# A hybrid encoder layer on one core: rounding copies on another engine, two rows from another ring, and one function table

## The chip, the cores and the metric

The kernel runs on one core of a Trainium2 chip, as one launch. The metric is the device time in microseconds (us) of that core. The kernel before was run three times: 2490.52 us is the median, 2490.19 the lowest and 2495.68 the highest. One more execution was taken with the hardware profiler; its rows are what the text argues from.

A core has five engines with a queue each, and each queue issues its instructions in order: TensorE (PE; its weight loads are listed as PEld), VectorE (DVE), ScalarE (ACT), GpSimd (POOL) and SyncE (SP, which here only starts transfers). An instruction that waits holds up everything behind it in its own queue.

## The reference, cut to what matters

One layer is applied to 1024 new rows (a prompt) and to 64 rows that continue a stream with a cache. The width is 1024.

```python
xn = rmsnorm(x); proj = xn @ w_in          # z | xBC | dt | q | k | v | g_ssm | g_att
y  = SSD_scan(silu(conv(xBC)), dt)         # 32 heads of 64, state 128, 4 groups
y  = rmsnorm_per_group(y * silu(z))
o  = subln(diff_attention(q, k, v))
x  = x + (sig(g_ssm) * (y @ W_bs) + sig(g_att) * (o @ W_ba)) @ W_out
h  = rmsnorm(x) @ w_up; ha, hb = split(h)  # 2 x 2816
x  = x + (silu(conv(ha)) * hb) @ w_down
```

Everything is float32. Keys, values, states and the convolutions' last rows are returned as well.

## The kernel before, in words

**Numbers in two parts.** All operands of the large products are kept as a high part `hi` (the value rounded to fp32r, the float32 form that PE multiplies at its fast rate) and a low part `lo` (value minus `hi`). A product of 128x128 blocks is three matmuls: hi x hi, hi x lo, lo x hi (`product`, L145 to L150). So each operand that is not a weight already on the way needs a rounding copy and a subtraction. `weights` (L130 to L142) loads a block of 128x1024, rounds it on ACT (L141) and subtracts on DVE (L142).

**Layout.** Channels lie on the partitions; the 1088 rows (1024 + 64) lie along the free axis, in three stretches `WIDE` of 384, 384 and 320 columns.

**Stages, in time.** 1. RMSNorm of x, then v and dt. 2. q and k. 3. Attention, head by head; between its steps the generator `filler` runs pieces of other work: the projections of z, xBC with its convolution, and the gates (`stream`, in the order `ORDER`, the gates 1 and 0 last). 4. The scan (`scan`, 4 groups by three stretches), with the rest of `filler` and then `branch_tiles` between its steps. 5. The second half of the state-space branch, then the output projection and the second norm. 6. The feed-forward part.

**The branches** (`branch`, L184 on). A branch product takes eight row tiles of 128 channels as the right operand, for each of the three stretches, and eight output tiles m, in the turns `TURNS`. The right operand is made by `branch_rows` (L161): for attention both parts come from DRAM ready-made; for the state-space branch each of the eight tiles is loaded into a staging row (L171), rounded into `b_hi` on ACT (L172) and subtracted into `b_lo` on DVE (L173). The state-space branch has two halves of 1024 channels. The first half is multiplied during the scan; ACT copies each accumulator out (L197, `b_g`) and ACT's own queue starts its store into `n_sc`. The second half's rows (y_sc[D:]) exist only after the scan; `last_rows(x)` calls `branch_rows` for stretch x just after the first half has used that stretch for the last time, since `b_hi` and `b_lo` have one buffer for each stretch. Loaded rows, the neighbours read for the sums (gates, `n_sc`, `m_sc`; L180) and the copied accumulators share one ring `b_r` of 11 rows of 128x384. There are three accumulators in turn in the scan, one "mx" and two "mm", and only the two "mm" after it.

**The norm after the scan.** For each group and stretch `gated` multiplies y by z (POOL, L735), ACT squares, POOL adds; `normed` sums over partitions on PE, and `rstd_of` (L221 to L225) makes the reciprocal root with Ln, Exp and Square on ACT. y then goes to `y_sc` by a store in SP's queue (L751). The same helper serves every norm, the second one (`norm`, L892 on) too.

**Function tables.** ACT evaluates functions from a set of tables that is loaded beforehand. The program loads one by hand at the start (L246, the set that holds both Ln and Exp); the compiler puts further loads wherever the set in place lacks the next function. Tanh serves the gates (L431), z and the convolution, Silu the feed-forward part (L1079).

**The feed-forward part** splits each product into quarters and needs seven products of sums instead of eight. The right operands (PARTS) come from `first_differences` and `last_differences`; the left ones from `left_parts` (L945): two loaded blocks of weights give four quarters q11, q12, q21, q22; POOL makes the sums s1 (L955), s2 (L956), q11 - q21 (L966) and q12 - s2 (L973); each of the seven is split on ACT (L860) and DVE (L861). Two column halves s = 0, 1 are handled alike. Tiles 0 and 1 are computed plainly (`pair_plain`), while the differences are made; tile 2 is the first with seven products (`pair`), and it takes them in the order 0, 2, 1, 3, 4, 5, 6. Its left operands are made at once by `left_of(2)`; those of each later tile are made step by step while the one before it is multiplied.

Rows of 128x544 come from rings: "fa" and "fb" of 8 rows, "fu" 4, "fp" 3, "fs" and "fh" 2. The normed x1 fills "fa" (quarters 0 and 2, which make half s = 0) and "fb" (quarters 1 and 3). Then "fs" holds the pair t2 of each half in `last_differences`, and after it the sums `ws1`, `ws2`; "fa" takes the split quarters `wh`, `wl`, eight rows for one tile.

**What sets the order.** The order of instructions in each queue isn't written out: a planner runs the whole program on simulated engines, takes what is ready by the order in which it was written (with a bonus for `tc.high_priority`), gives out the rows of the rings as they come free, and fixes the queues. A change in one place can so alter the order of everything behind it.

Of the kernel before, what the change touches and what calls it, by code (L numbers as in the profile page):

```python
# [11 lines left out]
AF = mybir.ActivationFunctionType  # L12
# [6 lines left out]
D = 1024  # L19
# [10 lines left out]
FT = DFF // P  # L30
NORM = (128, 256, 192, 192, 192, 128)
LN_EXP = "natural_log_exp_and_others"
# [43 lines left out]
def hybrid_layer(ctx: ExitStack, tc: tile.TileContext, xT, prm, cst, rope, wvd, win, wbs, wba, wout, wup, wdn,  # L76
                 ckT, cv, st0, yT, kT, v, ssm, conv, ffn):
    nc = tc.nc
    V, S, G, PE = nc.vector, nc.scalar, nc.gpsimd, nc.tensor
    act = S.activation  # L80
# [5 lines left out]
    def scratch(name, shape, dt=F32):  # L86
        return dram.tile(shape, dt, name=name, tag=name)
# [5 lines left out]
    o_sc, y_sc = scratch("o_sc", [2 * D, T]), scratch("y_sc", [2 * D, T])  # L93
# [58 lines left out]
    def project(block, evac):  # L152
        w_hi, w_lo = weights(block, KT, P)
        for (c, w), (hi, lo) in zip(WIDE, xn):
            ps = acc(w)
            product(ps, [(w_hi[:, k], w_lo[:, k], hi[:, k], lo[:, k]) for k in range(KT)])
            with tc.high_priority(quick or ahead):
                evac(ps, c, w)
            yield

    def branch_rows(stage, src, x):  # L161

        c, w = WIDE[x]
        hi, lo = (xn_pool.tile([P, KT, w], R32, name=f"b_{u}{x}", tag=f"{u}{x}") for u in ("hi", "lo"))
        for k in range(8):
            if stage is None:
                for u, t in enumerate((hi, lo)):
                    load(out=t[:, k].bitcast(F32), in_=src[D * u + P * k : D * u + P * (k + 1), c : c + w])
            else:
                t = stage()[:, :w]  # L170
                load(out=t, in_=src[P * k : P * (k + 1), c : c + w])  # L171
                S.copy(hi[:, k], t)  # L172
                V.tensor_tensor(out=lo[:, k], in0=t, in1=hi[:, k], op=ALU.subtract)  # L173
        return hi, lo

    def neighbours(side, gates, adds, m, c, w):
        tiles = []
        for d, r0 in ([(g_sc, gates)] if gates is not None else []) + [(d, 0) for d in adds]:
            t = side()[:, :w]
            load(out=t, in_=d[r0 + P * m : r0 + P * (m + 1), c : c + w])  # L180
            tiles.append(t)
        return tiles

    def branch(stage, side, src, wts, gates, adds, out, parts=None, loaded=None, then=None):  # L184

        parts = parts or [branch_rows(stage, src, x) for x in range(3)]
        for ms in TURNS:
            wt = [weights(wts[m], KT, P) for m in ms]
            for x, ((c, w), (hi, lo)) in enumerate(zip(WIDE, parts)):
                for m, (w_hi, w_lo) in zip(ms, wt):  # L190
                    beside = (loaded or {}).get((m, x)) or neighbours(side, gates, adds, m, c, w)
                    to = beside[0] if beside else side()[:, :w]
                    ps = acc(w)
                    product(ps, [(w_hi[:, k], w_lo[:, k], hi[:, k], lo[:, k]) for k in range(KT)])
                    with tc.high_priority(ahead):
                        if not beside:
                            S.copy(to, ps)  # L197
                        elif not adds:
                            V.scalar_tensor_tensor(to, to, 1.0, ps, ALU.add, ALU.mult)
                        else:  # L200
                            V.tensor_tensor(out=beside[1], in0=beside[1], in1=ps, op=ALU.add)
                    if adds:
                        V.scalar_tensor_tensor(to, to, 1.0, beside[1], ALU.add, ALU.mult)
                        V.tensor_tensor(out=to, in0=to, in1=beside[2], op=ALU.add)
                    out(m, c, to)
                    if then is not None and (m, ms) == (7, TURNS[-1]):
                        then(x)
                    yield

    def store(dst, start=load):  # L210
        return lambda m, c, t: start(out=dst[P * m : P * (m + 1), c : c + t.shape[1]], in_=t)
# [22 lines left out]
    s1 = ExitStack()  # L234
# [3 lines left out]
    def stat(w):  # L238
        t = ps1.tile([P, 512], F32, name="st", tag="st", bufs=3)
        return t[:, :w]  # L240
# [4 lines left out]
    with tc.tile_pool(name="nx", bufs=1) as nx:  # L245
        S.preload_act_table_set(LN_EXP)  # L246
        c = 0
        for x, w in enumerate(NORM):
            xc = nx.tile([P, KT, max(NORM)], F32, name="xc", tag="xc", bufs=3)
            ps = stat(w)  # L250
# [17 lines left out]
            for k in range(KT):  # L268
                xr = nx.tile([P, max(NORM)], F32, name="nxr", tag="nxr", bufs=NXR)
                (G if k % 3 == 2 else V).tensor_tensor(out=xr[:, :w], in0=xc[:, k, :w], in1=rs[:, :w], op=ALU.mult)  # L270
                hi, lo = (t[:, k, c % 384 : c % 384 + w] for t in xn[c // 384])
# [4 lines left out]
    def staged(name):  # L276
        return st.tile([P, 384], F32, name=name, tag="zr", bufs=ZR)
# [27 lines left out]
    with tc.tile_pool(name="qk", bufs=1) as qk:  # L305
# [5 lines left out]
        def row(name, w=T):  # L311
            t = qk.tile([P, T], F32, name=name, tag="qr", bufs=QR)
            return t[:, :w]
# [110 lines left out]
    extra = None  # L424
    cv_pool = tc.alloc_tile_pool(name="cv", bufs=1, side="right")

    def gate_tiles(tiles):
        for j in tiles:
            def evac(ps, c, w):
                gt = staged("gt")[:, :w]  # L430
                act(gt, ps, AF.Tanh, scale=0.5)  # L431
                load(out=g_sc[P * j : P * (j + 1), c : c + w], in_=gt)

            yield from project(win[B_G + j], evac)
# [44 lines left out]
    def stream():  # L479
        for kind, which in ORDER:  # L480
            yield from {"c": conv_tiles, "z": z_tiles, "g": gate_tiles}[kind](which)
        two = [gate_tiles([j]) for j in (1, 0)]
        for _ in WIDE:
            for u in two:
                yield next(u)
# [176 lines left out]
    with (tc.tile_pool(name="sin", bufs=1) as sin, tc.tile_pool(name="sp", bufs=1) as sp,  # L662
# [125 lines left out]
        def stage():  # L788
            return bs.tile([P, 384], F32, name="b_f", tag="b_r", bufs=BR)
# [3 lines left out]

        def branch_tiles():
            nonlocal bs
            cv_pool.release()
            st.release()
            bs = tc.alloc_tile_pool(name="bs", bufs=1, side="right")
            yield from branch(None, side, o_sc, wba, D, (), store(m_sc))
            yield from branch(stage, side, y_sc[:D], wbs[0], None, (), store(n_sc, S.dma_start), then=last_rows)  # L800

        def last_rows(x):
            assert scanned
            parts.append(branch_rows(stage, y_sc[D:], x))
            if x == 0:
                for m in TURNS[0]:
                    loaded[m, 0] = neighbours(side, 0, (n_sc, m_sc), m, *WIDE[0])

        parts, loaded, scanned = [], {}, False
        bs, late = None, chain(filler, branch_tiles())  # L810
        for i in scan():
            if i == BRANCH_AT and late is not None:
# [46 lines left out]
    def split(hi, lo, src):  # L859
        S.copy(hi, src)  # L860
        V.tensor_tensor(out=lo, in0=src, in1=hi, op=ALU.subtract)  # L861
# [80 lines left out]
            w.append((hi, lo))  # L942
        return w

    def left_parts(blocks):  # L945

        n = blocks[0].shape[1] // 2
        a = []
        for block in blocks:
            w = wp.tile([P, WMAX], F32, name="w_f", tag="w_f", bufs=2)  # L950
            load(out=w[:, : 2 * n], in_=block)
            a += [w[:, :n], w[:, n : 2 * n]]
        q11, q12, q21, q22 = a
        s1, s2 = (row("fs", name)[:, :n] for name in ("ws1", "ws2"))
        G.tensor_tensor(out=s1, in0=q21, in1=q22, op=ALU.add)  # L955
        G.tensor_tensor(out=s2, in0=s1, in1=q11, op=ALU.subtract)  # L956

        def own(src):
            hi, lo = (row("fa", name, R32)[:, :n] for name in ("wh", "wl"))
            split(hi, lo, src)  # L960
            return hi, lo

        yield own(q11)
        yield own(s2)
        yield own(q12)
        G.tensor_tensor(out=q21, in0=q11, in1=q21, op=ALU.subtract)  # L966
        yield own(q21)
        t = [wp.tile([P, WMAX], R32, name=name, tag=name, bufs=2) for name in ("w_hi", "w_lo")]
        for i, src in enumerate((s1, q22)):
            hi, lo = (x[:, 512 * i : 512 * i + n] for x in t)  # L970
            split(hi, lo, src)
            yield hi, lo
        G.tensor_tensor(out=s2, in0=q12, in1=s2, op=ALU.subtract)  # L973
        hi, lo = (wp.tile([P, WMAX], R32, name=name, tag=name, bufs=2)[:, :n] for name in ("w_hi", "w_lo"))
        split(hi, lo, s2)
        yield hi, lo
# [1 line left out]
    DOWN_AT = [sum(DOWN[:g]) for g in range(len(DOWN))]  # L978
    work = [(None, f) for f in range(FT)] + [(g, j) for g in range(len(DOWN)) for j in range(4)]

    def left_of(i):
        g, f = work[i]
        if g is None:
            return left_parts([wup[f], wup[f + FT]])
        n, o = P * DOWN[g], 1024 * DOWN_AT[g]
        return left_parts([wdn[:, o + n * m : o + n * (m + 1)] for m in (2 * f, 2 * f + 1)])

# [18 lines left out]
    left = {}  # L1006
# [229 lines left out]
        next(u)  # L1236
    for s in range(2):
        last_differences(s)
    left[2] = list(left_of(2))
    for u in pairs:  # L1240
        next(u)
    for i, (g, f) in enumerate(work[2:], 2):
# [123 lines left out]
```

## Time and profile before

| | |
|---|---|
| median of three runs | 2490.52 us (2490.19 to 2495.68) |
| profiled execution | 2488.03 us, of which the span from first to last instruction is 2486.2 us |
| PE busy | 2436.3 us, 98% of the span |
| DVE busy | 1589.3 us, 64% |
| ACT busy | 1181.0 us, 48% |
| POOL busy | 692.3 us, 28% |
| mean granted clock of PE | 0.996 |

How to read it: busy times are sums over the span; an engine that is idle while another one is the bound costs nothing. Names such as `mm<-b_hi,w_hi` stand for a tile written and the tiles read. L148 is line 148 of the kernel. A row of waits names who waited and for whom, with the total, the number and the longest. PEclk is the share of PE's full clock that was granted.

### The profile page before, as it was taken

How to read it: one execution, taken by the hardware profiler on the slowest of the kernel's cores; microseconds unless marked ns; L12 is line 12 of the kernel's file. 1: busy time of each engine (PE TensorE's matmuls, PEld its weight loads, DVE VectorE, ACT ScalarE, POOL GpSimd, SP SyncE). 2: the span in 40 equal slices, each digit the busy share in tenths (PEclk: the TensorE clock that was granted, in tenths of full speed). 3: DMA queues.
4: the chain of work that ended last, by engine and by line, in shares of the span. 5: the costliest groups of instructions: out<-in, count | busy, mean ns of one | idle time of the engine just before them, and what ended most of it. 6: DMA issues, size and time to landing. Idle time of an engine off the chain costs nothing. (4 is left out here: it accounts for less than half of the span.)

```text
span 2486.2 us, 44728 instructions
## 1 busy us (share of the span) xinstructions
PE 2436.3 (98%) x16958; PEld 2356.2 (95%) x16958; DVE 1589.3 (64%) x2735; ACT 1181.0 (48%) x2564; POOL 692.3 (28%) x712
## 2 busy tenths in 40 slices
PE   8999999999999999999999999999999999999999
PEld 7999999999999999998888899999999999999998
DVE  7326254865777667537666774655687777677765
ACT  6234343644565555437656663325543333344441
POOL 3000000000111001005324332003466666666435
PEclk9999999999999999999999999999999999999999
DMA  5217249454354353254688753655234333458874
GB/s 166 78 56 273 81 181 285 138 163 135 125 150 131 117 155 115 93 186 157 205 271 299 233 182 137 215 179 179 73 110 150 115 133 123 141 180 226 222 175 160
DMA packets 272152, 403.62 MB, mean 162 GB/s; under 512 B 32544, under 2 KB 206240, under 8 KB 271808
## 3 DMA queue, kind: packets, MB, share of 16 engines
q1 hardware_dynamic: 263872, 387.39, 48.2%
q0 software_dynamic: 4608, 8.91, 2.3%
q10 hardware_dynamic: 3456, 4.46, 0.5%
q8 instruction: 133, 2.18, 0.4%
q14 instruction: 83, 0.68, 0.1%
HBM read 267.11 MB, written 133.56 MB: 161 GB/s over the span
## 5 line engine op out<-in xcount | busy, mean ns | idle before, releaser
L148 PE MATMUL mm<-xn_hi,w_hi 128*128 128x384 f32 (+1 forms) x1416 | 469.9, 332 | 0.9 <-DVE zr L441 0.9
L150 PE MATMUL mm<-xn_hi,w_lo 128*128 128x384 f32 (+1 forms) x1416 | 467.7, 330 | 0.5 <-DVE w_lo L142 0.5
L149 PE MATMUL mm<-xn_lo,w_hi 128*128 128x384 f32 (+1 forms) x1416 | 466.5, 329 | 0.0
L148 PEld LDWEIGHTS mm<-xn_hi,w_hi 128*128 128x128 f32 x1416 | 266.2, 188 | 5.3 <-issue 2.0
L150 PEld LDWEIGHTS mm<-xn_hi,w_lo 128*128 128x128 f32 x1416 | 266.1, 188 | 2.9 <-issue 0.8
L149 PEld LDWEIGHTS mm<-xn_lo,w_hi 128*128 128x128 f32 x1416 | 266.2, 188 | 1.8 <-issue 0.6
L142 DVE TENSOR_TENSOR w_lo<-w_f,w_hi 128x1024 fp32r<-128x1024 f32 (+1 forms) x120 | 152.4, 1271 | 116.7 <-ACT w_hi L141 116.3
L1057 PE MATMUL mx<-n,wh 128*128 128x272 f32 x1092 | 209.0, 288 | 1.6 <-ACT u L1193 0.9
L1057 PE MATMUL mx<-m,w_hi 128*128 128x272 f32 x1050 | 201.8, 289 | 5.4 <-DVE down L1207 3.4
L141 ACT CAST w_hi<-w_f 128x1024 fp32r<-128x1024 f32 (+1 forms) x120 | 125.8, 1049 | 123.1 <-PE mm L149 68.5
L1057 PEld LDWEIGHTS mx<-n,wh 128*128 128x128 f32 x1092 | 171.4, 188 | 2.2 <-ACT u L1193 1.4
L1057 PEld LDWEIGHTS mx<-m,w_hi 128*128 128x128 f32 x1050 | 166.3, 190 | 6.3 <-DVE down L1207 4.1
L1057 PE MATMUL mx<-n,wl 128*128 128x272 f32 x546 | 157.2, 289 | 0.0
L148 PE MATMUL mm<-b_hi,w_hi 128*128 128x384 f32 (+1 forms) x448 | 147.9, 330 | 6.2 <-ACT b_g L197 6.2
L1057 PE MATMUL mx<-m,w_lo 128*128 128x272 f32 x525 | 151.9, 289 | 0.0
L150 PE MATMUL mm<-b_hi,w_lo 128*128 128x384 f32 (+1 forms) x448 | 146.5, 327 | 0.0
L149 PE MATMUL mm<-b_lo,w_hi 128*128 128x384 f32 (+1 forms) x448 | 146.3, 327 | 0.0
L559 ACT ACTIVATE p_t<-sc,mx 128x1024 f32<-128x1024 f32 (+5 forms) x144 | 106.1, 739 | 74.9 <-DVE mx L550 37.0
L470 DVE SCALAR_TENSOR_TENSOR cc<-pre,par,cc 128x384 f32<-128x384 f32 (+1 forms) x216 | 126.5, 586 | 23.7 <-ACT cc L468 18.6
L458 POOL COPY pre<-pre 128x3 f32<-128x3 f32 x48 | 13.2, 274 | 454.6 <-ACT pre L459 333.9
L860 ACT CAST w_hi<-ws 128x512 fp32r<-128x512 f32 (+1 forms) x64 | 38.9, 607 | 156.6 <-PE mx L1057 102.8
L697 POOL TENSOR_SCALAR_AFFINE_SELECT bc<-bc 128x1024 f32<-128x1024 f32 (+1 forms) x36 | 40.0, 1111 | 260.1 <-ACT e L684 260.1
(375 smaller groups left out, 6747.6 us busy)
## 6 DMA issues: line engine op xcount, KB each, us to landing
w_f<-in_win_dram SPq DMA_DIRECT2D x76, 512.0 KB, 3.7
w_f<-in_wup_dram SPq DMA_DIRECT2D x44, 512.0 KB, 3.6
hr<-q_sc SPq DMA_DIRECT2D x70, 272.0 KB, 4.3
bc<-a_sc SPq DMA_DIRECT2D x32, 512.0 KB, 6.2
q_sc<-hb SPq DMA_DIRECT2D x44, 272.0 KB, 2.3
gb<-q_sc SPq DMA_DIRECT2D x44, 272.0 KB, 4.0
x_sc<-cc SPq DMA_DIRECT2D x48, 192.0 KB, 2.0
q_sc<-gb SPq DMA_DIRECT2D x33, 272.0 KB, 2.3
```

Of the source, the lines that this page charges most:

```text
L141: S.copy(hi, w)
L142: V.tensor_tensor(out=lo, in0=w, in1=hi, op=ALU.subtract)
L148: PE.matmul(ps, a_hi, b_hi, start=i == 0, stop=False)
L149: PE.matmul(ps, a_hi, b_lo, start=False, stop=False)
L150: PE.matmul(ps, a_lo, b_hi, start=False, stop=i == n - 1)
L458: G.tensor_copy(pre[:, 0:3], tail)
L470: V.scalar_tensor_tensor(cc[:, :m], pre[:, i : i + m], cw(i), cc[:, :m], ALU.mult, ALU.add)
L559: act(p_t[:n, :nk], sc[c][:n, :nk], AF.Exp, bias=mx[:n, c : c + 1], accum_out=dst)
L697: G.affine_select(bc[:L, :, :L], bc[:L, :, :L], [[0, 8], [1, L]], ALU.is_ge, -1e30, base=0, channel_multiplier=-1)
L860: S.copy(hi, src)
L1057: PE.matmul(ps, w[x][:, c], b[y][:, k], start=start and k == t == 0, stop=k == nk - 1 and t == 2, skip_group_check=not start)
```

## The change

Three edits, all of which bear on work behind the last gate:

1. `branch_rows` gets the engine's copy as a parameter. `last_rows` passes POOL's, so that the 24 rounding copies of the second half's rows run on POOL. The subtractions stay on DVE.
2. `left_of` and `left_parts` get the ring of the sums `ws1`, `ws2` as a parameter. For tile 2 the sums take rows of "fa" instead of "fs". All later tiles still use "fs".
3. `gate_tiles` remembers its last Tanh. The first step of `branch_tiles` loads the set with Ln and Exp, ordered behind that Tanh in ACT's queue.

```diff
-    def branch_rows(stage, src, x):
+    def branch_rows(stage, src, x, copy=S.copy):
...
-                S.copy(hi[:, k], t)
+                copy(hi[:, k], t)
                 V.tensor_tensor(out=lo[:, k], in0=t, in1=hi[:, k], op=ALU.subtract)
...
+    last_gate = None
+
     def gate_tiles(tiles):
         for j in tiles:
             def evac(ps, c, w):
+                nonlocal last_gate
                 gt = staged("gt")[:, :w]
-                act(gt, ps, AF.Tanh, scale=0.5)
+                last_gate = act(gt, ps, AF.Tanh, scale=0.5)
...
         def branch_tiles():
             nonlocal bs
+            with tc.issue_after(last_gate.ins):
+                S.preload_act_table_set(LN_EXP)
             cv_pool.release()
...
-            parts.append(branch_rows(stage, y_sc[D:], x))
+            parts.append(branch_rows(stage, y_sc[D:], x, G.tensor_copy))
...
-    def left_parts(blocks):
+    def left_parts(blocks, tag="fs"):
...
-        s1, s2 = (row("fs", name)[:, :n] for name in ("ws1", "ws2"))
+        s1, s2 = (row(tag, name)[:, :n] for name in ("ws1", "ws2"))
...
-    def left_of(i):
+    def left_of(i, tag="fs"):
         g, f = work[i]
         if g is None:
-            return left_parts([wup[f], wup[f + FT]])
+            return left_parts([wup[f], wup[f + FT]], tag)
...
-    left[2] = list(left_of(2))
+    left[2] = list(left_of(2, "fa"))
```

## The prediction

> **What bounds the kernel now.** I read the page first, then who TensorE (PE) waited for behind 1280 us, then the granted clock around the longest of these waits, then the queue of the engine that was waited for.
>
> ```profile
> span 2486.2 us, 44728 instructions
> PE 2436.3 (98%) x16958; PEld 2356.2 (95%) x16958; DVE 1589.3 (64%) x2735; ACT 1181.0 (48%) x2564; POOL 692.3 (28%) x712
> ```
>
> PE is busy for 98% of the span, so the time is PE's work plus 50 us in which it stands still. Work taken off ScalarE (ACT, 48%) or put on GpSimd (POOL, 28%) counts only where it ends one of those standstills. All three edits take effect behind 1280 us, where the last gate is evaluated. The waits of PE from there to 1860 us (who waited for whom, total, times, longest):
>
> ```profile
> PE mm L148 <- ACT b_g L197: 6.2, 2, 5.5
> PE mx L148 <- ACT w_hi L141: 3.0, 2, 2.8
> PE mm L1057 <- ACT w_hi L860: 3.0, 1, 3.0
> PE mx L150 <- DVE w_lo L142: 3.0, 3, 1.3
> PE mm L150 <- DVE w_lo L142: 1.4, 1, 1.4
> PE st L894 <- DVE n L224: 1.1, 1, 1.1
> PE mm L1115 <- ACT u L1122: 0.7, 1, 0.7
> ```
>
> A standstill costs more than its length. Stretches at and behind the three longest (length; busy us of PE, PEld, DVE, ACT, POOL; granted clock; DMA share; GB/s):
>
> ```profile
> 1557.00:1562.50 5.50, 0.02 (x1) 0.00 (x0) 4.43 (x8) 4.05 (x8) 0.00 (x0) 0.93 0.75 239
> 1562.50:1569.70 7.20, 7.18 (x25) 7.18 (x26) 2.31 (x6) 2.17 (x5) 0.00 (x0) 0.58 0.64 217
> 1575.00:1580.00 5.00, 5.00 (x31) 5.00 (x30) 4.24 (x11) 1.05 (x4) 0.00 (x0) 1.00 0.90 286
> 1815.00:1818.00 3.00, 0.04 (x1) 0.04 (x1) 0.94 (x2) 1.00 (x2) 2.92 (x4) 0.95 0.26 93
> 1818.00:1822.60 4.60, 4.60 (x25) 4.60 (x26) 4.46 (x4) 1.76 (x3) 3.96 (x3) 0.66 0.00 0
> 1424.30:1429.00 4.70, 0.65 (x4) 0.30 (x3) 3.41 (x5) 4.67 (x10) 4.04 (x3) 0.96 1.05 385
> 1429.00:1436.00 7.00, 7.00 (x43) 6.63 (x43) 7.00 (x9) 6.64 (x18) 2.23 (x2) 0.79 1.00 311
> ```
>
> The reader is to see PEclk drop to 0.58, 0.66 and 0.79 right behind the standstills, where 25 matmuls take 7.2 us instead of the 4.0 that the pace of 31 in 5 us gives. Lost on top: 7.2 x 0.42 = 3.0 us, 4.6 x 0.34 = 1.6 us, 7.0 x 0.21 = 1.5 us.
>
> **Edit 1, the 24 high parts on POOL.** They are 16 of 128x384 and 8 of 128x320. ACT's queue in time (start, us, times):
>
> ```profile
> 1546.43 1.03 ACT L172 CAST b_hi<-b_f 128x384 fp32r<-128x384 f32 x2 [4.47 <-DMA b_f<-y_sc]
> ...
> 1552.72 0.47 ACT L197 COPY b_g<-mm 128x384 f32<-128x384 f32 x1
> ...
> 1561.63 0.51 ACT L172 CAST b_hi<-b_f 128x384 fp32r<-128x384 f32 x1 [0.40 <-DMA b_f<-y_sc]
> 1562.05 0.42 ACT L197 COPY b_g<-mm 128x320 f32<-128x320 f32 x1
> ```
>
> The copies b_g (L197) empty the accumulators. They stand in ACT's in-order queue behind casts that wait for loads, one after the other; PE stops at 1557.0 because both "mm" banks are full and starts 0.5 us behind the copy of 1562.05. Without the casts that copy can run when its product ends. ACT loses, and POOL gets, these casts:
>
> ```profile
> L172 ACT CAST b_hi<-b_f 128x384 fp32r<-128x384 f32 x32 | 15.8, 511 | 18.9 <-DMA b_f<-y_sc 18.7
> L221 ACT ACT_TABLE_LOAD x12 | 15.4, 1283 | 0.2
> L222 ACT ACT_TABLE_LOAD x12 | 15.4, 1283 | 0.2
> ```
>
> No row shows POOL casting to fp32r. The nearest rows of one input, and the splits that follow on VectorE (DVE):
>
> ```profile
> L697 POOL TENSOR_SCALAR_AFFINE_SELECT bc<-bc 128x1024 f32<-128x1024 f32 x32 | 37.4, 1168 | 222.9 <-ACT e L684 222.9
> ...
> L1069 POOL COPY pre<-par 128x2 f32<-128x2 f32 x22 | 6.7, 306 | 24.8 <-DVE cc L1078 24.8
> ...
> L697 POOL TENSOR_SCALAR_AFFINE_SELECT bc<-bc 64x512 f32<-64x512 f32 x4 | 2.6, 653 | 37.2 <-ACT e L684 37.2
> ```
>
> ```profile
> 1805.50 2.43 POOL L1069 COPY pre<-par 128x2 f32<-128x2 f32 x1 [3.76 <-DVE cc L1078]
> ```
>
> ```profile
> L173 DVE TENSOR_TENSOR b_lo<-b_f,b_hi 128x384 fp32r<-128x384 f32 x16 | 8.6, 557 | 11.6 <-ACT b_hi L172 11.6
> ```
>
> From L697, (1168 - 653)/512 = 1.0 ns an element and 0.14 us fixed: an estimate of 0.52 us for 384, against 0.51 on ACT. The other end is 2.43 us, a two-element copy. I take 0.52, because it is nearest in form. If each cast and its split never overlap, a tile takes 0.52 + 0.56 = 1.08 us, 24 take 26 us. Edit 3 lets the casts begin 2.6 us sooner, at 1543.8, so the last tile is ready at 1570; PE, going on at 1557.0, asks for the last third four blocks of 24 later (3.9 us each at 31 in 5 us), at 1572.6. So the slower chain is covered, by 2.6 us. POOL has nothing else here (0.00 busy in the windows above), so nothing queues behind the new waits there; on DVE the splits now wait for POOL instead of ACT, with the products' sums (L201) behind them as before. SP's loads are the same.
> To gain: 6.2 of wait and 3.0 of clock, 9.2 at most, nothing at least. I leave 1.5, about the size of the small waits in the list, for the copy's own wait for a free staging row: **-7.7**.
>
> A rule of the Trainium skill speaks against this edit: "GPSIMD Engine Reference" (§ 1 Specifications, § 4.1) advises VectorE for elementwise work, and says that GpSimd contends with Vector instructions that have two SBUF inputs. The split is such an instruction, and the 2.43 us row agrees; by the rule the term goes towards the slower rival below.
>
> **Edit 2, the sums in "fa" rows.** At 1815 PE waits for w_hi (L860), the split of the sum ws. Rows of POOL, then of DVE:
>
> ```profile
> 1814.01 2.03 POOL L1084 TENSOR_TENSOR hb<-hb,cc 128x480 f32<-128x480 f32 x2 [0.53 <-ACT cc L1079]
> 1816.00 1.26 POOL L955 TENSOR_TENSOR ws<-w_f 128x512 f32<-128x512 f32 x1
> ```
>
> ```profile
> 1813.51 2.37 DVE L861 TENSOR_TENSOR m<-t,m 128x544 fp32r<-128x544 f32 x2
> ```
>
> The "fs" ring has two rows, and the t2 pair of the second half holds both until DVE's m<-t,m (1813.51 to 1815.88). Only then can L955 write ws. "fa" rows held only tiles of the first half (x1 of quarters 0 and 2), whose differences and splits come before these. The two additions (2 x 1.26 us on POOL) and their splits then lie beside the plain pairs. The new cost: ten tiles now share eight rows, so the q21 pair waits for a sum's or q11's row. q11's products are the first of pair 2 and q21's the fourth, so two sets of 24 matmuls (25 in 4.6 us even at that clock) cover it; without that cover it costs one cast and split, about 1.2 us. To gain: 3.0 + 1.6 = 4.6; nothing if the planner leaves the additions behind L1084. I take **-4.5**, since the row alone explains the date.
>
> **Edit 3, the function table.** The 24 loads shown (L221, L222) go, 30.8 us of ACT, and one comes. That the preload holds is seen at the start, where ACT's only table load of the first 335 us is this one, with Ln and Exp of six norms behind it:
>
> ```profile
> L246 ACT ACT_TABLE_LOAD x1 | 1.3, 1283 | 0.7 <-PEq L1354 0.7
> ```
>
> The new load lies on ACT at about 1280, with PE fed by the gates' projections: nothing; at worst 1.3 us. On a path the loads count by pairs, 2.6 us in each norm's chain:
>
> ```profile
> 1401.77 1.28 ACT L221 ACT_TABLE_LOAD   x1
> 1403.07 0.62 ACT L221 ACTIVATE gn<-grs,eps_t 128x384 f32<-128x384 f32 x1
> ```
>
> ```profile
> SPq L751 <- DVE y L750: 39.9, 5, 11.8
> ```
>
> The store of y (L751) holds SP's queue, 11.8 us at the longest, and the branch's loads stand behind it. Those loads feed the chain that leaves w_hi late at 1424: 2.6 us sooner, the 2.8 us wait shrinks to 0.2 and the half clock (1.5) goes; the 1.3 us for w_lo stays: **-4.1**, bounds 0 and -5.6. In the norms of x1 the waits of 1.4 (w_lo behind the scaling), 1.1 (n) and 0.7 (u) are each shorter than 2.6 us and hang on the same chain: **-3.2**, bounds 0 and -3.2.
>
> The page "ScalarE: Activation LUTs" of the Trainium skill (§ What ACT_TABLE_LOAD costs) gives 2.66 us for a switch, drain included. The trace differs: the ACTIVATE starts 1.30 us after the load did. By the page's figure the 1.3 us for w_lo would go as well, 1.3 us more.
>
> **Sum.** -7.7 - 4.5 - 4.1 - 3.2 = -19.5. Against it: the planner orders everything behind 1280 us anew from its own simulated times, and this order's waits were not in its plan either. I allow one new standstill like that of 1424, 4.1 + 1.5 = 5.6. Net -14. The profiled execution took 2488.0 us (span 2486.2 and 1.8 around it), so 2474; the median of the runs is 2490.5, 2.5 higher, so 2476.5 for a median. I give 2476. These runs spread over 0.2%, so I call 0.3% (7.5 us) the least change that can be told.
>
> **The rivals.**
> *The staging rows, not ACT, hold the copy.* Eleven rows serve loads, neighbours and the copies' results, and the copy of 1562.05 needs one that a split frees. For: the casts around it waited for loads. Against: the copy of 1552.72 was late as well. Edit 1 then gives only the 2.6 us of earlier loads: -2.6 - 4.5 - 4.1 - 3.2 + 5.6 = -8.8, 2482.
> *Slower: the casts starve on POOL.* Casts behind back-to-back DVE pairs take c each; the third column stretch is then ready at 1543.8 + 24c. Before, PE reached it at 1569.7 + 3 x 3.9 = 1581.4, so from c = 1.57 us edit 1 loses. At 2.43 us it is ready at 1602, 21 us late; with the others, 21 - 11.8 + 5.6 = +15, 2505. Slower overall by 7.5 us from c = 2.1. Against: the mean of L1069 is 0.31 us.
> *The plan gives it back.* Three or four new standstills of 5.6 us: 2488 to 2496. For: the 11 waits of the list arose under such a plan. Against: what stood in the way at the two longest is taken away by name.
> *The table is not kept.* If a Tanh comes behind the preload, edit 3 does nothing: -7.7 - 4.5 + 5.6 = -6.6, 2484.
>
> **How the numbers follow.** Forecast 0.53; staging rows 0.15; plan 0.18 (a third of it slower); table 0.06; starving 0.08. Faster by over 0.3%: the forecast and most of the staging case, 0.66. Same: the rest of it, the table, two thirds of the plan, 0.20. Slower: 0.14. The forecast's own range is 2468 to 2483; with the rivals up to the plan's upper part, 2466 to 2494, leaving out the starving case and a gain of all 19.5 with more.
>
> **What would show it.** Edit 1: POOL COPY b_hi x24 at about 0.5 us, no PE wait for b_g, clock 1.00 at 1560. Edit 2: L955 for pair 2 before 1800, no wait for w_hi L860 of 3 us. Edit 3: no ACT_TABLE_LOAD between the gates and the first Silu. Wrong if casts take over 1.5 us, if b_g still waits behind 1557, or if new PE waits over 2.5 us with half clock appear.

## The result, and the profile after

The changed kernel takes **2478.78 us** (median; 2475.05 to 2484.31) against 2490.36 us for the kernel before on the same chip (2486.90 to 2495.68): a ratio of 0.9953, with a 95% interval of 0.9938 to 0.9969. That is 11.6 us or 0.47% faster; the forecast was 2476 with a range of 2466 to 2494. The profiled execution took 2477.45 us, close to its median, where that of before took 2488.03, 2.3 us under its own.

The total came out nearly as forecast. Its terms did not: edit 3 alone brings all of the gain, and edit 1, the largest term, costs time. Most of what follows is about that. Page of the changed kernel, then its waits of PE from 1280 to 1860 us (who waited for whom, total, times, longest):

```profile
span 2475.7 us, 44723 instructions
PE 2433.8 (98%) x16958; PEld 2355.8 (95%) x16958; DVE 1596.5 (64%) x2735; ACT 1139.1 (46%) x2517; POOL 705.2 (28%) x736
```
```profile
PE mm L148 <- ACT b_g L197: 6.2, 1, 6.2
PE mx L150 <- DVE w_lo L142: 3.2, 2, 2.0
PE mx L1120 <- ACT u L1127: 2.4, 1, 2.4
PE mx L148 <- ACT w_hi L141: 0.6, 1, 0.6
```

ACT lost 42 us of work and POOL gained 13, and neither is what set the time. The wait for b_g, which edit 1 was to end, is 6.2 us as it was. The 3.0 us for w_hi at pair 2 is gone, and so are the three small waits in the norms; but a new wait of 2.4 us for u has come. (Lines behind the diff are shifted by 3 to 5: L860 is now L865, L861 L866, L955 and L956 L960 and L961, L1115 L1120, L1122 L1127.)

To see where the time went I compared the start of the same matmul in two traces: both kernels run 16958 of them, in the same order but for at most 214 of them in any kernel, and no cut point below lies among those. The difference of these starts, taken between fixed matmuls, gives the gain of each stage. The columns, by the times of before: up to 1369 us; 1369 to 1492 (the scan's wait at 1424); 1492 to 1629 (the waits for b_g); 1629 to 1793 (output and norms of x1); 1793 to 1899 (pair 2's start); 1899 to the end. "Median" is that of all runs of the kernel, "ratio" is to the kernel before on the same chip.

| kernel | to 1369 | scan 1424 | b_g | norms | pair 2 | rest | median us | ratio, 95% interval |
|---|---|---|---|---|---|---|---|---|
| the change (1+2+3) | 1.6 | 1.3 | 1.6 | 1.2 | 5.1 | -0.9 | 2478.78 | 0.9953 (0.9938 to 0.9969) |
| edit 1 alone | -1.0 | -2.8 | -2.8 | 0.5 | -0.6 | 0.4 | 2491.33 | 1.0002 (0.9992 to 1.0011) |
| edit 2 alone | -1.3 | -2.4 | -1.2 | -3.8 | 5.1 | -1.4 | 2489.61 | 0.9995 (0.9986 to 1.0005) |
| edit 3 alone | -0.7 | 3.3 | 4.3 | 5.3 | 0.1 | -1.8 | 2476.97 | 0.9942 (0.9929 to 0.9955) |
| 2+3 | 1.5 | 4.1 | 3.6 | 1.8 | 5.1 | -4.4 | 2475.58 | 0.9945 (0.9933 to 0.9956) |
| 3, tables back in the last scan norm | 2.5 | 4.2 | 2.5 | 4.6 | 0.4 | -2.0 | 2478.91 | 0.9954 (0.9942 to 0.9967) |
| 1+2+3, neighbours last | 0.0 | 4.3 | 3.8 | -0.2 | 5.1 | -1.8 | 2475.49 | 0.9943 (0.9930 to 0.9957) |
| 1+2+3, sums ordered later | 2.8 | 3.9 | 1.3 | 4.6 | 2.2 | -5.2 | 2478.47 | 0.9959 (0.9946 to 0.9972) |
| rows alone | 3.3 | -3.0 | 9.4 | 0.8 | -0.6 | -1.8 | 2481.29 | 0.9967 (0.9955 to 0.9979) |
| rows, 3 | 0.4 | 3.1 | 9.4 | 5.3 | 0.5 | -2.0 | 2471.03 | 0.9921 (0.9907 to 0.9936) |
| rows, 2+3 | 0.6 | 3.9 | 9.4 | 3.7 | 3.7 | -4.7 | 2471.41 | 0.9929 (0.9916 to 0.9942) |
| rows, 1+2+3 | 0.9 | 3.2 | 7.8 | 2.8 | 3.8 | -2.2 | 2472.44 | 0.9924 (0.9910 to 0.9937) |
| rows, 2+3, sums ordered later | -2.6 | 2.2 | 9.4 | 5.3 | 2.7 | -3.2 | 2471.82 | 0.9923 (0.9911 to 0.9936) |

The first column is the size of chance in these rows: nothing of the edits lies there but one table load, and it runs from -2.6 to +3.3. What a stage gives is trusted where several rows agree on it.

### The profile page after: what moved, and what is told of

Read it like the earlier page. It is cut to its first block, busy times and chain, and to the rows that moved or that the text cites. A ratio compares the mean times of both kernels' runs of the same rounds, so it can differ in the third digit from the quotient of the medians.

```text
span 2475.7 us, 44723 instructions
## 1 busy us (share of the span) xinstructions
PE 2433.8 (98%) x16958; PEld 2355.8 (95%) x16958; DVE 1596.5 (64%) x2735; ACT 1139.1 (46%) x2517; POOL 705.2 (28%) x736
## 3 DMA queue, kind: packets, MB, share of 16 engines
q8 instruction: 133, 2.18, 0.4%
## 4 chain that ended last, share of the span: by engine, by line
PE 69%; DMA 4%; DVE 4%; ACT 2%; issue 2%; SPq 1%; POOL 0%; DVEq 0%; ACTq 0%; POOLq 0%
PE mx L1062 17%; PE mm L148 9%; PE mm L150 9%; PE mm L149 9%; PE mm L1062 7%; PE po L596 3%; PE mx L150 2%; PE mx L148 2%; PE mx L149 2%; PE sc L549 1%; PE sc L548 1%; PE pt L577 1%; PE mx L1120 1%; PE ye L717 1%; PE yi L711 1%
## 5 line engine op out<-in xcount | busy, mean ns | idle before, releaser
L865 ACT CAST w_hi<-ws 128x512 fp32r<-128x512 f32 (+1 forms) x64 | 38.9, 608 | 158.6 <-PE mx L1062 112.9
```

## The experiments

### Each edit alone

Edit 1 alone has only the copy argument of the diff, edit 2 alone only the ring tag, edit 3 alone only `last_gate` and the preload.

> Edit 1 alone on the kernel before (the 24 copies b_hi of the second half's rows on GpSimd, nothing else). Theory A, the prediction's: ScalarE's queue held the copies b_g of the first half, so the 6.2 us wait of PE for b_g and most of the slow clock behind it go: -7.7 us, about 2482.7. Theory B, the rival: the last copies b_g wait for a row of the ring of 11 that the splits of the second half's rows set free; the wait stays at 5 to 6.5 us, and only the shorter first block remains of the gain, as between the two traces (1.7 us): -1 to -2.6, 2488 to 2489.5.

2491.33 us, ratio 1.0002 (0.9992 to 1.0011): no change. Its waits of PE from 1280 us on begin:

```profile
PE mm L148 <- ACT b_g L197: 10.2, 1, 10.2
PE mx L148 <- ACT w_hi L141: 4.0, 2, 3.7
```

The wait for b_g did not shrink but grew, from 6.2 (in two pieces) to 10.2. Theory A fails: taking the 24 casts off ACT's queue does not free the copies.

> Edit 2 alone (ws1 and ws2 of pair 2 in the ring fa). Theory A, the prediction's: the 3.0 us wait for w_hi at pair 2's start and its slow clock go: -4.5, about 2486. Theory B: the sums, now run earlier on GpSimd, fall beside the splits of VectorE under the norms and bring the 2.4 us wait of PE for u near 1772 with its slow clock of about 1.5 us; then the 4.6 us that the two traces show at pair 2's start are paid back by up to 3.9: -0.7 to -2.5, 2488 to 2490, and the new wait stands in this trace and not in that of edit 3 alone.

2489.61 us, ratio 0.9995 (0.9986 to 1.0005). Theory B: pair 2's start gains 5.1, and the norms lose 3.8 to the new wait, which stands in this trace and not in that of edit 3 alone:

```profile
PE mx L1115 <- ACT u L1122: 2.8, 1, 2.8
```

> Edit 3 alone (the table with Ln and Exp loaded after the last gate's Tanh). Theory A, the prediction's: -4.1 in the scan and -3.2 in the norms: about 2483. Theory B: in the scan only 1.3 goes, because the wait passes on to w_lo and the slow clock stays, and the norms give their 3.3 (the 2.4 us wait near 1772 belongs to edit 2 and is not here): -4.6, about 2486. Theory C: the wait near 1772 comes from the shorter norms and stands here too: -1.3 to -2.5, 2488 to 2489.

2476.97 us, ratio 0.9942 (0.9929 to 0.9955), below what any of the three theories gave: edit 3 alone is as fast as the whole change. Its waits of PE from 1280 us on:

```profile
PE mm L148 <- ACT b_g L197: 3.4, 1, 3.4
PE mm L1062 <- ACT w_hi L865: 2.5, 1, 2.5
PE mx L150 <- DVE w_lo L142: 1.8, 2, 1.2
PE mx L148 <- DVE b_g L199: 1.4, 1, 1.4
PE mx L148 <- ACT w_hi L141: 1.0, 1, 1.0
PE mm L1062 <- DVE hb L1163: 0.6, 1, 0.6
```

The wait for b_g, which no theory gave to edit 3, went from 6.2 to 3.4, and the waits in the norms are gone without the 2.4 us for u.

### The change without edit 1

Edits 2 and 3; `last_rows` calls `branch_rows(stage, y_sc[D:], x)` as before.

> The changed kernel without edit 1 (the casts of the second half's rows back on ScalarE). By the single edits (edit 3 alone 2477.0 with a 3.4 us wait for b_g, edit 2 alone about -1.2) edit 1 costs some 2.7 us in the changed kernel: 2475 to 2476.5, with PE's wait for b_g at about 3.4 us in place of 6.2. By the prediction's term (edit 1 gains up to 7.7) it is 2486, by the rival of the staging rows (2.6) 2481.

2475.58 us, and the wait for b_g is 4.2 us against 6.2 with edit 1. Edit 1 so costs 3.2 us by the medians and 2.0 by the ratios (0.9945 and 0.9953). The two intervals overlap, so the time alone doesn't show it, but the wait moves the same way here and in edit 1 alone, and so does the stage (3.6 against 1.6).

### What held the copies: rows of their own

The staged rows b_f of the second half leave the ring of 11 (b_r) for tiles that the scan has done with, four or six rows in each:

```
+        own = []
+        def own_row():
+            if not own:
+                for pool, tag, n, k in ((sin, "in", 2, 6), (sin, "zin", 2, 4), (sp, "y", 2, 4)):
+                    for _ in range(n):
+                        t = pool.tile([P, k, 384], F32, name="b_o", tag=tag, bufs=n)
+                        own.extend(t[:, j] for j in range(k))
+            return own.pop(0)
...
-            parts.append(branch_rows(stage, y_sc[D:], x, G.tensor_copy))
+            parts.append(branch_rows(own_row, y_sc[D:], x, G.tensor_copy))
```

> The changed kernel, with the 24 staged rows b_f of the second half in rows of their own (the scan's finished tiles) in place of the ring of 11 that they share with b_g. Theory B (the ring holds the copies b_g): the copies of the last products run when their products end, the 6.2 us wait of PE for b_g and the slow clock of some 3 us behind it go, with up to 2 us late next: -7 to -9 against the changed kernel, 2470 to 2472. Theory A (the order on ScalarE's queue holds them, whatever the rows do): the wait stays at about 6 us, 2479 as the changed kernel. A third: the copies run but PE then waits for the split of the second half's first rows, for 2 to 5 us: 2473 to 2477.

2472.44 us, 6.3 under the changed kernel: Theory B by its mechanism, since no wait for a copy b_g on ACT is left, and a little short of its 7 to 9. The three kernels that follow have the same rows with other edits: edits 2 and 3 with the casts on ACT, none of the edits, and edit 3 alone.

> The kernel with rows of their own for the second half's staging, and the casts back on ScalarE (edits 2 and 3 and the rows). Theory R (only rows held the copies b_g): the copies run on time here as well, no wait of PE for b_g above 1 us, 2471.5 to 2473.5 as with the casts on GpSimd (2472.4). Theory A (ScalarE's queue holds them as well, once the rows are free): PE waits 2 to 6 us for b_g with a slow clock behind it, 2475 to 2479.

2471.41 us: Theory R. With the casts on ACT and the rows free, the copies run on time. The stage gains 9.4 here and 7.8 with the casts on POOL, so by these traces the casts are cheaper on ACT even where no row is short.

> The kernel before with the rows of their own, and none of the three edits. Theory R: in the kernel before too the ring of rows held the copies b_g, and ScalarE's casts did not; the waits for b_g (6.2 us) and the slow clock behind go as with edit 3 beside them: -8 to -9.4, 2481 to 2482.5, and edit 3 on top of it is worth the scan's 3.3 and the norms' 5.3. Theory A: with the table loads of the last norm and the casts still on ScalarE's queue, PE goes on waiting for b_g for 2 to 6 us: 2485 to 2490.

2481.29 us, 8.7 us under the kernel before (ratio 0.9967, 0.9955 to 0.9979): Theory R. This is the plainest test of edit 1's term, since ACT has the same casts and table loads in its queue as before. The casts now find their rows loaded, so they don't hold the queue up either. Edit 1 alone shows that clearing the queue is not enough; this kernel shows that freeing the rows is. The stretch 1540 to 1580 us (length; busy us of PE, PEld, DVE, ACT, POOL; granted clock; DMA share; GB/s) in the kernel before, in the changed kernel, and with rows alone:

```profile
1540.00:1580.00 40.00, 33.84 (x186) 33.31 (x185) 21.89 (x44) 16.52 (x35) 0.00 (x0) 0.91 0.79 258
```
```profile
1540.00:1580.00 40.00, 33.78 (x197) 33.51 (x197) 25.94 (x45) 6.20 (x14) 14.48 (x24) 0.91 0.79 255
```
```profile
1540.00:1580.00 40.00, 40.00 (x247) 40.00 (x247) 27.52 (x57) 18.08 (x43) 0.00 (x0) 1.00 0.64 204
```

The edit moved 10 us of work from ACT to POOL and left PE and the clock as they were. The rows left ACT alone, and PE runs through at full clock, with 247 matmuls in place of 186.

> Edit 3 and the rows of their own, without edits 1 and 2. Theory: with the rows the wait for b_g is gone, and edit 2 is worth only its net of about 1.2 (5.1 at pair 2's start, less 3.9 in the norms): 2472 to 2473.5, with a wait of 2.5 to 3 us for w_hi at pair 2's start and none for u in the norms. By the prediction's term (4.5) it is 2475.5 to 2476.5.

2471.03 us, the lowest median here, 7.8 us under the changed kernel and 1 below what the theory gave. The wait for w_hi at pair 2's start is there (2.3 us), and still edit 2, which removes it, makes nothing of it: 2471.41 with it. At pair 2's start itself edit 2 gains 3.2 (3.7 against 0.5); the norms and the rest take it back.

### Why edit 1 costs: who gets the rows

ACT's order around the copies in the changed kernel (start, us, idle before and what ended it):

```profile
1545.60 0.48 ACT L197 COPY b_g<-mm 128x384 f32<-128x384 f32 x1 [6.49 <-DVE b_lo L173]
...
1546.56 0.48 ACT L197 COPY b_g<-mx 128x384 f32<-128x384 f32 x1 [0.47 <-DVE b_lo L173]
...
1559.00 0.42 ACT L197 COPY b_g<-mm 128x320 f32<-128x320 f32 x1 [4.81 <-DVE b_lo L173]
```

ACT is idle before each of these copies, and a split (b_lo) ends the wait: the copy has no row to write to. With no casts ahead of them on ACT, the first two copies take the first rows that the splits set free, and the staged rows of the next column stretch wait until such a copy is stored. SP's queue, of the changed kernel and then of edit 3 alone:

```profile
1544.82 0.38 SPq L180 DMA_DIRECT2D b_g<-m_sc  x1
1550.48 1.43 SPq L171 DMA_DIRECT2D b_f<-y_sc  x3
```
```profile
1545.62 0.38 SPq L180 DMA_DIRECT2D b_g<-m_sc  x1
1546.52 6.56 SPq L171 DMA_DIRECT2D b_f<-y_sc  x6
```

In the changed kernel no staged row is loaded from 1545.2 to 1550.48; with the casts on ACT the loads go on at 1546.52, 4.0 us earlier. The copy of 1559.00 waits for a split of that stretch. That the loads wait for the copies' stores can be read from SP's own waits. These are its waits before a load of a staged row (L171) for a store of a copy (n_sc<-b_g), from 1535 to 1572 us: before, edit 1 alone, edits 2 and 3, and the changed kernel.

```profile
SPq L171 <- DMA n_sc<-b_g: 5.3, 2, 2.7
```
```profile
SPq L171 <- DMA n_sc<-b_g: 10.0, 2, 5.5
```
```profile
SPq L171 <- DMA n_sc<-b_g: 5.4, 3, 3.6
```
```profile
SPq L171 <- DMA n_sc<-b_g: 9.8, 3, 5.2
```

With edit 1 this wait is about twice as long, alone and beside the other two edits. It is not all of edit 1's cost: with rows of their own the casts on POOL still cost 1.6 us in this stage (7.8 against 9.4), where PE waits 1.1 us for results of VectorE (the sum of L201 and w_lo). How much of that is in the changed kernel's cost was not separated.

In the next kernel the six loads of neighbours (g_sc, n_sc, m_sc), which lie in the ring as well, are traced last:

```
-            if x == 0:
+            if x == 2:
                 for m in TURNS[0]:
                     loaded[m, 0] = neighbours(side, 0, (n_sc, m_sc), m, *WIDE[0])
```

> The changed kernel, with the rows g_sc, n_sc, m_sc of products 0 and 1 of the second half's first stretch traced behind the staged rows of all three stretches instead of behind the first. Theory R: in the changed kernel these six loads take the six free rows of the ring before the staged rows of stretch 1 get one; now those start some 4 us earlier, their splits set rows free earlier, and PE's wait for b_g falls from 6.2 to 3.4 us or less with half of its slow clock: -3 to -5, 2474 to 2476. Rival P: the casts on GpSimd, 0.83 us beside VectorE's splits where ScalarE took 0.51, are what is late: the wait stays at 5.5 us or more, 2478 to 2480. A third: PE waits at the second half's first product for the neighbours' rows: no PE wait for b_g, but one of VectorE and then of PE behind it, 2478 or more.

2475.49 us, the time of Theory R, by the path of the third theory: no wait for a copy b_g is left, but PE waits 3.7 us for the neighbours' sum.

```profile
PE mm L148 <- DVE b_g L201: 3.7, 1, 3.7
```
```profile
1536.06 12.79 SPq L171 DMA_DIRECT2D b_f<-y_sc  x16
```

Sixteen staged rows now load in a row. The rows are the limit in either order: what one user of the ring gains another pays, in part. One thing in the expectation was wrong: edit 3 alone loads the six neighbours early too, so they are a use of the ring, and not the difference that edit 1 makes. That difference is when the copies take their rows.

### Why edit 3 gave 4.3 us at b_g

The staged rows are loaded behind the last store of y (L754), and that store ends the scan's last norm. ACT in this norm, before, and with edit 3 alone:

```profile
1534.37 0.43 ACT L747 COPY grs<-gst 128x320 f32<-128x320 f32 x1 [1.25 <-PE gst L744]
1534.81 1.28 ACT L221 ACT_TABLE_LOAD   x1
1536.11 0.56 ACT L221 ACTIVATE gn<-grs,eps_t 128x320 f32<-128x320 f32 x1
1536.69 1.28 ACT L222 ACT_TABLE_LOAD   x1
1537.98 0.47 ACT L222 ACTIVATE gn<-gn 128x320 f32<-128x320 f32 x1
```
```profile
1531.76 0.43 ACT L750 COPY grs<-gst 128x320 f32<-128x320 f32 x1 [1.25 <-PE gst L747]
1532.21 0.57 ACT L221 ACTIVATE gn<-grs,eps_t 128x320 f32<-128x320 f32 x1
1532.81 0.47 ACT L222 ACTIVATE gn<-gn 128x320 f32<-128x320 f32 x1
```

And SP's queue at the end of it, before and then with edit 3 alone:

```profile
1542.50 0.37 SPq L751 DMA_DIRECT2D y_sc<-y  x1
```
```profile
1537.31 0.37 SPq L754 DMA_DIRECT2D y_sc<-y  x1
```

Behind the same copy grs the exponential begins 1.05 instead of 3.61 us later, and the store of y 5.55 instead of 8.13: both 2.6 us sooner. To test that this is the way, two loads are put back there and nowhere else:

```
             with tc.high_priority(ahead):
-                S.copy(rs, ps)
+                got_rs = S.copy(rs, ps)
+            if again:
+                with tc.issue_after(got_rs.ins):
+                    S.preload_act_table_set("sigmoid_and_others")
+                    S.preload_act_table_set(LN_EXP)
```

> Edit 3 alone, but with two table loads put back in the scan's last norm (between the copy grs and the Ln, 1.28 us each), nothing else. Theory T: the 4.3 us that edit 3 won around the second half's first product came through this norm: its y_sc store was 2.6 us earlier behind the copy, the loads of the staged rows stand behind that store on SP's queue, and so the rows and the last copies b_g came earlier. With the two loads back, PE's wait for b_g is 5.5 to 6.5 us instead of 3.4, and the time is 2.6 to 4.3 above edit 3 alone (2477.0): 2479.5 to 2481.5. Rival: the order of the work had changed for another reason and the norm has no part in it: the wait stays near 3.4 us, 2476.5 to 2478.

2478.91 us, 1.9 above edit 3 alone (the intervals overlap), and the wait for b_g is 4.7 instead of 3.4: between the two theories. The stage gives 2.5 instead of 4.3, so by these two traces some 1.8 of the 4.3 us come by this norm. The two loads also changed the order behind them (two casts and a copy change places on ACT), so the rest is left open. The Trainium skill, "ScalarE: Activation LUTs" (§ What ACT_TABLE_LOAD costs), gives 2.66 us for each switch, drain included; in this trace the two loads together end 2.57 us after the first began, and the logarithm starts 0.01 behind them, so a switch takes 1.28.

### The new wait in the norms

VectorE, then POOL, in the changed kernel ahead of the wait for u, with ACT's copy of u behind; then VectorE at the same work with edit 3 alone:

```profile
1766.89 1.88 DVE L866 TENSOR_TENSOR m<-x,m 128x544 fp32r<-128x544 f32 x1
1768.69 1.83 DVE L936 TENSOR_TENSOR x<-x,t 128x544 f32<-128x544 f32 x1
1770.44 1.81 DVE L866 TENSOR_TENSOR m<-x,m 128x544 fp32r<-128x544 f32 x1
1772.17 1.50 DVE L225 SCALAR_TENSOR_TENSOR n<-n,n 128x272 f32<-128x272 f32 x1
```
```profile
1768.14 1.79 POOL L960 TENSOR_TENSOR ws<-w_f 128x512 f32<-128x512 f32 x1
1770.01 1.66 POOL L961 TENSOR_TENSOR ws<-ws,w_f 128x512 f32<-128x512 f32 x1
1771.63 1.74 POOL L971 TENSOR_TENSOR w_f<-w_f 128x512 f32<-128x512 f32 x1
```
```profile
1773.70 0.39 ACT L1127 COPY u<-mx 128x272 f32<-128x272 f32 x1 [2.02 <-DVE n L225]
```
```profile
1766.03 0.71 DVE L936 TENSOR_TENSOR x<-x,t 128x544 f32<-128x544 f32 x1
1766.67 0.71 DVE L866 TENSOR_TENSOR m<-x,m 128x544 fp32r<-128x544 f32 x1
...
1767.91 0.43 DVE L225 SCALAR_TENSOR_TENSOR n<-n,n 128x272 f32<-128x272 f32 x1
```

Beside POOL's sums VectorE's instructions of 1768.69 and 1770.44 take 1.8 us instead of 0.71, and n takes 1.50 instead of 0.43, in all 3.3 us more. (The row of 1766.89 is slow mostly beside POOL's last difference, L932, which both kernels have and which ends at 1768.18 here.) ACT's copy of u waits 2.0 us until n is done, and PE waits for the copy. The test orders the sums on POOL behind the last differences:

```
-        last_differences(s)
-    left[2] = list(left_of(2, "fa"))
+        last = last_differences(s)
+    with tc.issue_after(last.ins):
+        left[2] = list(left_of(2, "fa"))
```

> The changed kernel, with the sums of pair 2 ordered on GpSimd behind the last difference L932 of the second column half. Theory S: the sums at 1768 to 1773 slowed VectorE's splits from 0.72 to 1.8 us, which made n (L225) late and PE wait 2.4 us for u; moved behind, they leave VectorE alone there, the wait and its slow clock of 1.5 to 1.7 us go, and pair 2 still finds its sums: -3.5 to -4.1, 2474.5 to 2475.5. Rival: the order of VectorE's queue alone delays n, so the wait stays: 2479. A third: the sums then fall beside the splits of the next norm, or are late for pair 2, with 1.2 to 3 us: 2476 to 2479.

The wait for u in the norms is gone, as Theory S has it, and the norms give 4.6 instead of 1.2; but the median is 2478.47, no gain. The third theory holds for the time: 2.9 go back at pair 2, where PE now waits 1.9 us for its u (L1154), and 4.3 in the rest. The last was not traced to a cause.

> Edits 2 and 3, the rows of their own, the casts on ScalarE, and pair 2's sums ordered behind the last differences. Theory: the wait for u in the norms (1.4 us and part of a slow clock) goes, pair 2's own wait for u stays below 2 us: 2469 to 2471. Rival, as the sums alone showed: the later sums are paid back at pair 2 and behind it: 2471 to 2472.5, no change against 2471.4.

2471.82 us: the rival. With the rows free the later sums make no difference either.

## Why the prediction was right in total and wrong in its terms

**Edit 1, -7.7: wrong, and of the wrong sign.** The step that failed is "Without the casts that copy can run when its product ends". The copies did stand behind casts in ACT's queue, but they also needed a row of the ring, and this was the gate that counted: rows alone, with every cast still on ACT, ended the wait (-8.7), and edit 1 alone left the time at 1.0002 of before. In the change it costs 2.0 (by the ratios) to 3.2 us (by the medians). The 1.5 us that I left "for the copy's own wait for a free staging row" became the whole wait, 6.2. By its own sign the term was wrong, since b_g still waits behind 1557. The rival of the staging rows had the mechanism (chance 0.15), but its price of -2.6 still took a gain from earlier loads; and what I held against it, that the copy of 1552.72 was late as well, is no evidence: in the changed kernel that copy and the next (1545.60, 1546.56) wait for rows as well. Of the slower chain only the pace was sized rightly. The casts took

```profile
L172 POOL CAST b_hi<-b_f 128x384 fp32r<-128x384 f32 x16 | 9.6, 622 | 25.6 <-DMA b_f<-y_sc 25.6
```

0.62 us on average against the 0.52 estimated, far from the 1.57 of the slower rival. The last cast ended at 1570.25, but a tile is ready only with its split, and the last split ended at 1574.5, where 1570 was forecast and PE was to ask at 1572.6. No wait of PE came of it in this trace, in which PE had stood still for 6.2 us before.

**Edit 2, -4.5: its gain right, its cost left out.** Pair 2's start gained 5.1 in all four kernels with edit 2, the ring of 11 and the sums left to the planner. The step that failed is that the additions and their splits "lie beside the plain pairs" for nothing: they lie beside VectorE's splits there, and cost the norms 3.5 to 4.1 us (5.3 with edit 3 alone, 1.8 with edits 2 and 3, 1.2 with all three). Alone it is worth 1.3 by the medians, within its interval nothing.

**Edit 3, -4.1 and -3.2: right, and too small.** All 24 loads went. In the scan the ten kernels with edit 3 gain 3.4 on average (1.3 to 4.3); the three others without it lose 2.4 to 3.0 against the profile of before, so that this profile was a lucky one there. Against the mean of all four without edit 3 (-2.1) the term is 5.4. The profile of the changed kernel is the lowest of the ten: the wait for w_hi shrank nearly as forecast (to 0.57 from 2.76, forecast 0.2), but the wait for w_lo grew to 2.05 and the slow clock stayed. The norms gave 4.6 to 5.3 instead of 3.2: of PE's waits there, 3.9 us in all before, none is left with edit 3 alone, two smaller ones (0.5 and 0.2) among them. The other 1.4 was not traced; it isn't the clock, which was 1.00 there before as well. What I left out is the scan's last norm: I priced the store of y only for the loads behind 1424, not for the staged rows at 1543, which gave 4.3 more in edit 3 alone. (The 2.6 us sooner stands in the prediction, but as the cover of edit 1.)

**The allowance of +5.6** for one new standstill was about right in kind: the change brought one, of 2.4 us with 7 us at a clock of 0.76 behind it (1.7 us), in all 4.1.

**The sum.** By the medians, edit 3 is worth -13.9, edit 2 on top of it -1.4 (2475.58 less 2476.97) and edit 1 on top of both +3.2: -12.1, against 11.6 measured. By the ratios, each to its own runs of the kernel before, they are -14.4, +0.7 and +2.0. So edit 3 brings all of the gain, and edit 2 on top of it can't be told from nothing. Forecast were -7.3, -4.5, -7.7 and +5.6: -14. Too much for the one edit and too little for another cancelled: that the total came out is luck, and by the edits' own terms the forecast is not borne out.

## What to carry to other kernels

Where an engine's instruction waits in an in-order queue, look also at the buffer that it writes: an instruction has two gates, and taking away the one seen in the queue gains nothing if the ring of rows is the later one. More than that, an instruction that comes free early takes a row early, and so can make others late. And a chain that is shortened by a fixed piece (a table load twice in a norm) is to be followed to every wait behind it, not only to the nearest.

## What the runs showed of the hardware

- **VectorE and POOL slow each other.** VectorE's two-input instructions of 128x544 take 0.71 us alone and 1.81 to 1.88 beside POOL's two-input ones (the sums, the last difference). POOL's cast of 128x384 took 0.51 us alone and 0.83 alternating with the splits, and these 0.55 and 0.85. The Trainium skill, "GPSIMD Engine Reference" (§ 1 Specifications), says that the two contend when a Vector instruction has two SBUF inputs; the traces agree, and the 2.5-fold price is theirs.
- **The granted clock is 1.00 or 0.50, and how long a standstill lowers it is not sharp.** A fall lasts 3.4 or 6.8 us in these traces (10.2 once, in edit 1 alone), so it costs up to 1.7 or 3.4 us of PE's work; a mean such as 0.77 over 7 us is one fall of 3.4. In the kernel before, behind the wait for b_g:

```profile
1561.80:1568.50 6.70, 5.98 (x19) 5.98 (x20) 2.33 (x5) 2.24 (x6) 0.00 (x0) 0.50 0.69 244
```

  From 1280 to 1900 us, the mean clock of the 7 us behind standstills of 2.3 us and more was 0.51 to 0.79 in all but one. Below that, both occur: 0.76 behind 1.73 and 1.87 us and 0.77 behind 2.05, but 1.00 behind 1.80, 1.95, 2.18 and 2.28; and while it was 1.00 behind those of 1.34 to 1.59 us, it fell to half behind one of 1.15 (1301.7 us, neighbours last). Nor do these bounds hold elsewhere in the span: 0.76 behind 1.38 us (623.8 us, "rows, 2+3, sums ordered later"), but 1.00 behind 2.89 (1216 us, edit 2 alone). The Trainium skill, "TensorE: Matmul & The Clock Gate" (§ Part 1: The HAM clock gate), has the clock fall to half after an idle window of some 3.4 us, with windows that run free. The traces agree on the half and on 3.4 us as the length of a fall, but show it behind standstills of half that length and less. A window that runs free would fit a bound that is not sharp, which no run here shows. Three rows from the changed kernel (behind its 2.05, 6.2 and 2.4 us), and one from edit 3 alone at the scan's wait, where two standstills of 1.0 and 1.2 us with matmuls between left the clock alone:

```profile
1426.00:1433.00 7.00, 6.94 (x42) 6.63 (x42) 7.00 (x10) 6.03 (x15) 1.77 (x2) 0.77 0.85 256
1559.50:1566.50 7.00, 7.00 (x33) 7.00 (x34) 3.82 (x6) 0.42 (x1) 3.63 (x7) 0.79 0.67 217
1774.00:1781.00 7.00, 6.86 (x43) 6.86 (x44) 7.00 (x15) 4.72 (x12) 2.11 (x1) 0.76 0.00 1
```
```profile
1429.00:1434.00 5.00, 5.00 (x43) 4.63 (x42) 5.00 (x8) 5.00 (x13) 1.44 (x1) 1.00 1.00 285
```

- **Some of each gain goes back at the end.** From 1899 us on, where no edit acts, every kernel but edit 1 alone loses 0.9 to 5.2 us against the trace of before. The waits of PE that grow there are for VectorE's `down` (L1207 of before) and ScalarE's `u` (L1193): 4.9 and 2.9 us with edits 2 and 3, against 3.9 and 0.9 before. Why was not settled.
